# A layer with a matrix scan on one core: the block solver's loads, places and priority, and products between merge pieces

## The chip, the cores and the metric

The kernel runs on one core of a Trainium2 chip. The core has TensorE (PE, with its weight loads as PEld), VectorE (DVE), ScalarE (ACT), GpSimd (POOL) and SyncE (SP), which here only issues transfers; 16 DMA engines move the data. The metric is the device time of one execution in microseconds.

## The reference

One layer over 1024 latent tokens and 256 context tokens of width 1024, all in 32-bit floats:

```
h  = modulate(rms_norm(x, norm1_g), sh1, sc1)          # also for the context
u  = h @ w_in                                           # 512 Fourier columns, 1920 RWKV columns
r, k, v = conv1d_centred(u[rkv]); decay, a = low-rank maps; kk = normalised k
for each time step, direction and head (2 x 8, state 64 x 64):
    sa = s @ kk_t
    s  = s * w_t - sa kk_t a_t + v_t k_t
    y  = s @ r_t                                        # context tokens first, no readout there
rw  = (group_norm(y) + bonus) * gate
out = concat(fourier_mix(u[:512]), rw) @ w_out;  x = x + g1 * out
h2  = modulate(rms_norm(x, norm2_g), sh2, sc2)
x   = x + g2 * (silu(gate) * val) @ w_down              # gate, val = 3x3 grid convolution of h2 @ w_up
return rms_norm(x, final_g)
```

The scan over time is a chain: a state depends on the one before.

## The kernel before, in words

**Scan in chunks.** The 1280 time steps are cut into 20 chunks of 64 (the first four are the context), worked as `step(s)` for s = 0 to 19, each over 16 pairs of direction and head. Inside a chunk the recurrence is a triangular system. Its inverse `z` (64 x 64 a chunk and pair) is found outside the chain, for a *block* of four chunks at a time: `solve(b)` inverts the 32 x 32 diagonal parts on VectorE, with 128 of them side by side, one in each partition, by 30 rounds of two instructions (L853, L854); `merge(b)` puts the two 32 x 32 halves together on PE in four pieces (two at L874, two at L883), each read out by ScalarE (L877, L886). Blocks 0 to 4 serve steps 0-3, 4-7 and so on. `prep(s)` (L939) applies `z` to the inputs of step s. A step is: `pw` (L957), its copy (L959), `py` (L964), `pS` (L973), the state update on VectorE (add L975, multiply L977), the second part of `py` (L982). Between them stand the two halves of `prep(s+1)`.

**The solver's data.** The preparation writes the scores to DRAM (`xad`), rows first. `solve(b)` loads them into `n` with the row in the partition, by four transfers (L843, L844: rows of 64 or 32 floats); VectorE turns them (L848) into `arr`, where a partition holds one matrix; after the rounds it turns the inverse back twice (L858, L859). `n` alternates between two pools (`wks[b % 2]`); `arr` has one place, in `wks[0]`. `merge` needs `n` and `arr`.

**Preparation.** The input projection runs in products of 128 columns (`product`, L197, into `plat`, two places of two PSUM banks). After each, generators in `self.sides` hand out small pieces in turn, two a product part (`tick`): the norm of `k` (`norms`), the transposes of `v` (`turns`), and the pair work that makes the scan's inputs (`pair`, `scores`). Each yields a PE instruction; PE's order is the order of tracing here. The preparation has two PSUM pools one after the other (`s1a`, `s1b`), and `plat` is in both. The first solve is interleaved with the last pair by hand.

**What sets the order.** A planner orders each engine's instructions when the program is built: it runs a picture of time with its own costs and takes, among what is ready, what has the best priority; priority goes by the order of tracing unless `prio` shifts it. `behind(i)` and `paced` tie an instruction to stand behind another one on its own engine. In `weave` the scan's chain and a *fill* (the remaining Fourier products, then the Fourier transform and its output projection) are traced with a far better priority (`-AHEAD`), and PE's instructions of both are tied into one fixed order (`self.link`): the plan's numbers say how many fill pieces follow each step. In `chain` the next block's solver is traced a few rounds at a time behind the step's parts, with the same priority; in steps 2, 6, 10 (and 14) its rest is finished, and the merge pieces stand between the step's parts, with no fill between them.

**After the scan.** `heads_out` and `out_pieces` (with `second_norm`, which writes `h2` through `v2`, a small buffer of four places) run in steps 14 to 19; then come the feed-forward products (`ffn_up`, `down_round`).

Of the kernel before, what the change touches and what calls it, by code (L numbers as in the profile page):

```python
# [10 lines left out]
F32 = mybir.dt.float32  # L11
F32R = mybir.dt.float32r
AF = mybir.ActivationFunctionType
OP = mybir.AluOpType
# [149 lines left out]
class B:  # L164
# [63 lines left out]
    def weave(self, a, b, fill=(), plan=()):  # L228
# [5 lines left out]
        while True:  # L234
# [76 lines left out]
    def stage0(self, wk, hT, first, rest):  # L311
# [64 lines left out]
        us = [(pp.tile([128, T], F32, name="plat", bufs=2), pp.tile([128, TC], F32, name="pctx", bufs=2)) for m in first]  # L376
# [77 lines left out]
    def post_k(self, us, m):  # L454
# [7 lines left out]
        def norms():  # L462
            nc.scalar.activation(kk, k, AF.Square, scale=self.kk_[:, p:p + 1])
            for b, n in BLOCKS:
# [12 lines left out]
    def post_v(self, us, m):  # L477
        nc, wk = self.nc, self.wk
# [6 lines left out]

        def turns():
            for d in range(2):
                for b0 in (0, 4, 8):
                    nb = min(4, 10 - b0)
                    x = v[:, b0 * 128:(b0 + nb) * 128]  # L490
                    if d:
                        vr = wk.tile([128, 512], F32, name="vrev", tag="vt", bufs=2)
                        nc.vector.tensor_copy(vr[:, :nb * 128], rev(v[:, TT - (b0 + nb) * 128:TT - b0 * 128]))
                        x = vr
                    vt = wk.tile([128, 4, 128], F32, name="vt", bufs=2)
                    aux = self.pp.tile([128, 512], F32, name="aux")
                    for b in range(nb):
                        i = nc.tensor.transpose(aux[:, b * 128:(b + 1) * 128], x[:, b * 128:(b + 1) * 128], self.ident)
                    nc.scalar.activation(vt[:, :nb], aux[:, :nb * 128].rearrange("p (b c) -> p b c", c=128), AF.Copy)
                    t0 = b0 if d else (b0 + 2) % 10  # L500
                    for h in range(2):
                        nc.sync.dma_start(rows[d, h, :, t0:t0 + nb], vt[:, :nb, 64 * h:64 * h + 64])
                    yield i
# [191 lines left out]
    def fourier_first(self, hT):  # L695
# [5 lines left out]
        for j in range(2):  # L701
# [3 lines left out]
            us.append(self.pp.tile([128, T], F32, name="plat", bufs=2))  # L705
# [3 lines left out]
    def fourier_rest(self, hT, wk, us):  # L709
# [10 lines left out]
        for j in range(2, 4):  # L720
# [4 lines left out]
            ps = self.pp.tile([128, T], F32, name="plat", bufs=2)  # L725
# [99 lines left out]
    def gate_rows(self, pool):  # L825
# [5 lines left out]
        nc.gpsimd.tensor_add(gb, gb, t)  # L831
        return gb


    def solve(self, b):


# [665 lines left out]
```

## Time and profile before

| | |
|---|---|
| time, median of 3 runs | 1714.73 us (1708.97 to 1720.9) |
| profiled execution | 1714.45 us |
| its span, first to last instruction | 1712.7 us |
| instructions | 29106 |
| PE, PEld busy | 89%, 72% |
| VectorE, ScalarE, GpSimd busy | 66%, 41%, 30% |
| mean granted PE clock | 0.931 |
| DMA traffic | 246.29 MB in 208919 packets |

A busy share is that of the whole span. "L957" is line 957 of the kernel. A row such as "PE pw L957 <- DVE SV L977" says that PE sat idle ahead of line 957 until VectorE's line 977 released it. The granted clock is the share of full speed at which PE was let run. In a group, the columns after the bar are the busy time, the mean of one in ns, and the idle time just before.

### The profile page before, as it was taken

To read this page: it belongs to the slowest core of one execution; us is meant where nothing else is said; L and a number is where in the kernel's file an instruction comes from. 1 tells how busy PE (TensorE), PEld (TensorE's weight loads), DVE (VectorE), ACT (ScalarE), POOL (GpSimd) and SP (SyncE) were. 2 spreads that over 40 slices of the span, in tenths; PEclk is the share of its full clock that TensorE was granted. 3 is DMA by queue.
4 is the path that set the end of the run, shared out by engine and by line. 5 is a ranking of instruction groups with operands and counts; after the bars stand their busy time and mean duration, and the time that the engine had idled before them with its cause. 6 is when DMAs were issued, how large, how long until landed. Compare 5 with 4: busy or idle time off the path is not lost. (4 is left out here: it accounts for less than half of the span.)

```text
span 1712.7 us, 29106 instructions
## 1 busy us (share of the span) xinstructions
PE 1520.9 (89%) x11642; PEld 1229.8 (72%) x11642; DVE 1129.6 (66%) x1604; ACT 702.2 (41%) x1193; POOL 507.4 (30%) x443
## 2 busy tenths in 40 slices
PE   4998898888977768899897999999999998999996
PEld 3786676665656566778676888888888886787785
DVE  3614745665596685866557599999999999515613
ACT  3433545556443334423666422222222223435533
POOL 0013523443332134301215122222222223354454
PEclk7999998999988777789999999999999999999998
DMA  8577757767778667564620311111111115434532
GB/s 313 201 287 214 227 165 215 230 184 231 177 215 178 160 164 173 179 174 140 191 95 16 116 39 48 50 50 49 50 50 50 49 50 185 158 124 138 195 124 98
DMA packets 208919, 246.29 MB, mean 144 GB/s; under 512 B 53238, under 2 KB 162944, under 8 KB 208784
## 3 DMA queue, kind: packets, MB, share of 16 engines
q1 hardware_dynamic: 202608, 233.92, 45.1%
q0 software_dynamic: 6176, 10.51, 2.2%
q8 instruction: 92, 1.51, 0.4%
q14 instruction: 43, 0.35, 0.1%
HBM read 177.99 MB, written 66.33 MB: 143 GB/s over the span
## 5 line engine op out<-in xcount | busy, mean ns | idle before, releaser
L189 POOL TENSOR_TENSOR wlo<-wraw,whi 128x1024 fp32r<-128x1024 f32 x105 | 253.0, 2411 | 656.9 <-ACT whi L188 656.9
L1223 DVE SCALAR_TENSOR_TENSOR conv<-u,c_fcw,conv 128x945 f32<-128x945 f32 (+2 forms) x344 | 411.5, 1219 | 36.2 <-ACT conv L1216 28.1
L188 ACT ACTIVATE whi<-wraw 128x1024 fp32r<-128x1024 f32 x123 | 129.4, 1052 | 301.5 <-issue 165.8
L197 PE MATMUL u<-h2h,wlo 128*128 128x512 f32 x672 | 206.9, 389 | 0.0
L197 PE MATMUL u<-h2h,whi 128*128 128x512 f32 x672 | 206.9, 389 | 0.0
L197 PE MATMUL u<-h2l,whi 128*128 128x512 f32 x672 | 206.8, 389 | 0.0
L189 DVE TENSOR_TENSOR al<-act,ah 128x256 fp32r<-128x256 f32 (+1 forms) x88 | 62.7, 716 | 137.8 <-ACT ah L188 137.5
L197 PEld LDWEIGHTS u<-h2h,wlo 128*128 128x128 f32 x672 | 126.1, 188 | 26.2
L197 PEld LDWEIGHTS u<-h2l,whi 128*128 128x128 f32 x672 | 126.1, 188 | 26.1
L197 PEld LDWEIGHTS u<-h2h,whi 128*128 128x128 f32 x672 | 126.1, 188 | 26.2
L1280 PE MATMUL e<-wlo,ah 128*128 128x512 f32 x264 | 103.0, 390 | 2.8 <-POOL wlo L189 2.8
L197 PE MATMUL plat<-hTh,whi 128*128 128x512 f32 x272 | 99.6, 447 | 4.5 <-DVE v L451 4.5
L188 ACT ACTIVATE ah<-act 128x256 fp32r<-128x256 f32 (+1 forms) x88 | 45.9, 523 | 139.6 <-PE e L1280 99.3
L1280 PE MATMUL e<-whi,al 128*128 128x512 f32 x264 | 103.0, 390 | 0.0
L197 PE MATMUL plat<-hTl,whi 128*128 128x512 f32 x272 | 90.8, 415 | 0.0
L197 PE MATMUL plat<-hTh,wlo 128*128 128x512 f32 x272 | 90.0, 412 | 0.5 <-DVE wlo L668 0.5
L916 POOL COPY WV<-SV 64x512 f32<-64x512 f32 x40 | 26.6, 666 | 146.4 <-ACT xs L941 45.6
L1280 PE MATMUL e<-whi,ah 128*128 128x512 f32 x264 | 67.0, 389 | 0.0
L559 DVE TENSOR_TENSOR_SCAN cs<-c_rst,sg 128x256 f32<-128x256 f32 x40 | 31.0, 776 | 50.1 <-ACT sg L543 45.8
L197 PEld LDWEIGHTS plat<-hTh,wlo 128*128 128x128 f32 x272 | 53.6, 198 | 13.6 <-DVE wlo L668 0.9
L634 PEld LDWEIGHTS aux<-x,bk 64*128 64x128 f32 x640 | 46.1, 207 | 24.0 <-issue 12.5
L197 PEld LDWEIGHTS plat<-hTh,whi 128*128 128x128 f32 x272 | 47.1, 195 | 22.2 <-issue 14.1
(292 smaller groups left out, 3134.1 us busy)
## 6 DMA issues: line engine op xcount, KB each, us to landing
wraw<-wd SPq DMA_DIRECT2D x66, 512.0 KB
ad<-ada SPq DMA_DIRECT2D x12, 2048.0 KB
wraw<-wu SPq DMA_DIRECT2D x42, 512.0 KB
xrd<-x SPq DMA_DIRECT2D x32, 640.0 KB
xs<-xrd SPq DMA_DIRECT2D x16, 1280.0 KB
xad<-x SPq DMA_DIRECT2D x80, 192.0 KB
xs<-xad SPq DMA_DIRECT2D x18, 512.0 KB
kvb<-kvd SPq DMA_DIRECT2D x16, 512.0 KB
```

The lines of the kernel that those rows point to most:

```text
L188: self.nc.scalar.activation(hi, x, AF.Copy)
L189: (lo_eng or self.nc.gpsimd).tensor_sub(lo, x, hi.bitcast(F32))
L197: mm = self.nc.tensor.matmul(ps[:, b:b + n], wt[:, k, :], xt[:, k, b:b + n], start=k == 0 and i == 0, stop=k == 7 and i == 2)
L559: nc.vector.tensor_tensor_scan(cs, self.rst, o(sg), 0.0, op0=OP.mult, op1=OP.add)
L634: i = nc.tensor.matmul(ps[h][:, c, :64 * w], bk(c, h), x[R[h], c, 1:6 * w - 4:6], start=True, stop=True)
L916: nc.gpsimd.tensor_copy(wv[r, h], sv[r, h])
L1223: nc.vector.scalar_tensor_tensor(og[:, R, Cc], ug[:, Ri, Ci], self.fcw[:, m, w:w + 1], og[:, R, Cc], op0=OP.mult, op1=OP.add)
L1280: nc.tensor.matmul(t, x[:, 128 * (i - i0):128 * (i - i0) + 128], w[:, j, 512 * (b - b0):512 * (b - b0) + 512], start=k == 0 and m == 0, st ...
```

## The change

**Preparation.** `plat` moves to a PSUM pool of its own (`s1p`) that lives through both halves. `norms` hands over its turn once between the square and the first product. `turns` makes the reversed copy of the next piece before it works on the present one, and its buffers (`vt` and `vrev` together) have four places instead of two.

**Solver.** `arr` is loaded directly, one matrix in a partition, by four transfers with rows of 32 floats, and lies in `wks[b % 2]`, like `n`. The opening transpose is gone. After the rounds, `solved(b)` loads the part of `n` that `merge` still needs (two transfers) and does the two closing transposes. The loads of blocks 1 and 2 are traced between the input loads of steps 0, 1 and 2, those of block 3 at the end of step 2, and of block 4 at the end of step 6. `solving(b, i)` traces all rounds at once with a worse priority than all else (`+AHEAD // 2`), behind the update of step 0, 3 or 7 (block 1: at the chain's start).

**Merge steps.** After each merge piece of steps 2, 6 and 10 the chain says "mid", and `weave` puts the plan's next number of fill pieces there; the plan's sums are as before (19 and 52 pieces).

**Room.** `tab` has four places instead of six; the raw output weights are taken from the Fourier transform's pool; `v2` takes `arr`'s place in `wks[1]`, as one tile of four pieces.

```diff
-            if i == "end":
+            if i in ("mid", "end"):
                 self.burst(fill, next(plan, 0))
...
-        ul = self.pp.tile([128, T], F32, name="plat", bufs=2)
+        ul = self.pl.tile([128, T], F32, name="plat", bufs=2)
...
             nc.scalar.activation(kk, k, AF.Square, scale=self.kk_[:, p:p + 1])
+            yield self.pace[-1]
...
+        def turned(b0, nb):
+            vr = self.wv.tile([128, 512], F32, name="vrev", tag="vt", bufs=4)
+            nc.vector.tensor_copy(vr[:, :nb * 128], rev(v[:, TT - (b0 + nb) * 128:TT - b0 * 128]))
+            return vr
+
         def turns():
...
+            for j, (d, b0, nb) in enumerate(pieces):
+                x = vr if d else v[:, b0 * 128:(b0 + nb) * 128]
+                if j + 1 < len(pieces) and pieces[j + 1][0]:
+                    vr = turned(*pieces[j + 1][1:])
+                vt = self.wv.tile([128, 4, 128], F32, name="vt", bufs=4)
...
-                    tab = wk.tile([128, 2, 258], F32R, name="tab", bufs=6)
+                    tab = wk.tile([128, 2, 258], F32R, name="tab", bufs=4)
...
+    def solve_load(self, b):
+        src = self.xad[b].rearrange("p i q f -> (i q) p f")
+        arr = self.arrs[b] = self.wks[b % 2].tile([128, 32, 32], F32, name="arr")
+        for h in range(2):
+            for g in range(2):
+                r = slice(64 * h + 32 * g, 64 * h + 32 * g + 32)
+                self.nc.sync.dma_start(arr[r], src[:, r, 192 * h + 32 * g:192 * h + 32 * g + 32])
+
     def solve(self, b):
-        n = self.wks[b % 2].tile([128, 32, 64], F32, name="n")
...
-        diag = n[:, :, 0:32]
-        arr = self.wks[0].tile([128, 32, 32], F32, name="arr")
-        nc.vector.transpose(arr.rearrange("p a b -> p b a"), diag.rearrange("p m c -> p c m"))
+        nc, arr = self.nc, self.arrs[b]
         for j in range(1, 31):
...
+    def solved(self, b):
+        nc, arr = self.nc, self.arrs[b]
+        n = self.wks[b % 2].tile([128, 32, 64], F32, name="n")
+        src = self.xad[b].rearrange("p i q f -> p (i q) f")
+        for h in range(2):
+            nc.sync.dma_start(n[64 * h:64 * h + 32, :, 32:64], src[64 * h:64 * h + 32, :, 192 * h + 32:192 * h + 64])
+        diag = n[:, :, 0:32]
         nc.vector.transpose(diag.rearrange("p m c -> p c m"), arr)
         nc.vector.transpose(arr, diag)
...
+    def solving(self, b, i):
+        with self.prio(by=AHEAD // 2), self.behind(i):
+            for _ in self.solve(b):
+                pass
...
             yield from self.merge(0)
-            self.ahead = self.solve(1)
         for s in range(4) if not a else (4,) if a == 4 else ():
             self.load_x(s)
+            if s < 2:
+                self.solve_load(s + 1)
         if a in (0, 4):
             yield from self.prep(a)
+        if not a:
+            self.solving(1, None)
...
                 elif s % 4 == 2:
                     if not n:
-                        for _ in self.more:
-                            pass
+                        self.solved(g)
                         self.more = self.merge(g)
                     else:
-                        yield from islice(self.more, 1)
-                elif n >= late and left:
-                    left -= 1
-                    next(self.more, None)
-            for _ in range(left):
-                next(self.more, None)
+                        for i in islice(self.more, 1):
+                            yield i
+                            yield "mid"
             if s % 4 == 2 and s < 14:
-                yield from self.more
-                self.ahead = self.solve(g + 1)
-                next(self.ahead)
+                for i in self.more:
+                    yield i
+                    yield "mid"
+                if g < 3:
+                    self.solve_load(g + 2)
+            if s in (0, 3, 7):
+                self.solving(g + 1, self.updated)
             yield "end"
...
-            v = wk.tile([128, 2, 128], F32, name="v2", bufs=4)
+            if o % 4 == 0:
+                vs = self.wks[1].tile([128, 4, 2, 128], F32, name="v2", tag="arr")
+            v = vs[:, o % 4]
...
-                b.weave(0, 4, fill, (7, 6, 6))
+                b.weave(0, 4, fill, (7, 4, 4, 1, 1, 1, 1))
...
-            b.weave(4, 14, fill, (0, 0, 4, 5, 4, 5, 1, 8, 8, 9, 8))
+            b.weave(4, 14, fill, (0, 2, 3, 1, 1, 1, 1, 1, 4, 4, 1, 2, 2, 2, 2, 0, 8, 9, 8))
```

More of the change, by code (lines that the diff above doesn't have):

```diff
@@ L375, in stage0 @@
             modulation(q, ads[q])
-        us = [(pp.tile([128, T], F32, name="plat", bufs=2), pp.tile([128, TC], F32, name="pctx", bufs=2)) for m in first]
+        us = [(self.pl.tile([128, T], F32, name="plat", bufs=2), pp.tile([128, TC], F32, name="pctx", bufs=2)) for m in first]
         for n, (b, w) in enumerate(BLOCKS):
@@ L724, in fourier_rest @@
                 side.append(more)
-            ps = self.pp.tile([128, T], F32, name="plat", bufs=2)
+            ps = self.pl.tile([128, T], F32, name="plat", bufs=2)
             for k in range(8):
@@ L863, in solve, with first_solve @@
         self.zs[b] = n, arr
+    def first_solve(self):
+        self.solve_load(0)
+        yield
+        yield from self.solve(0)
+        self.solved(0)
     def merge(self, b):
@@ L999, in chain @@
             yield from self.merge(0)
-            self.ahead = self.solve(1)
         for s in range(4) if not a else (4,) if a == 4 else ():
             self.load_x(s)
+            if s < 2:
+                self.solve_load(s + 1)
         if a in (0, 4):
             yield from self.prep(a)
+        if not a:
+            self.solving(1, None)
         for s in range(a, b):
             g = (s + 1) // 4 + 1
-            if s in (0, 3, 7, 11):
-                self.more, self.share = self.ahead, 9 if not s else 6
-            late, left = 3 if s >= 4 else 2, self.share if s % 4 != 2 and s < 14 else 0
             if s > 14 and s % 2 == 0:
@@ L1062, in loads @@
                     yield
-        return w, loads()
+        return w, loads
     def out_pieces(self, w, hs, x, n):
@@ L1330, in build @@
             b.wp = pool("w", st)
+            b.pl = pool("s1p", st, space=PSUM)
             s1, s1k = ExitStack(), ExitStack()
@@ L1359, in build @@
                 b.bank = b.pp, "aux"
-                b.first = b.solve(0)
+                b.first = b.first_solve()
                 pairs = b.pairs()
@@ L1399, in fill @@
                 with ExitStack() as st:
-                    for n, i in enumerate(b.fourier_out(pool("fo", st, side="right"))):
+                    fo = pool("fo", st, side="right")
+                    parts = loads(fo)
+                    for n, i in enumerate(b.fourier_out(fo)):
                         yield i
                         if n % 2:
-                            next(loads, None)
-                b.out_all(loads)
+                            next(parts, None)
+                    b.out_all(parts)
                 x1 = b.x1 = pool("x1", tail, side="right").tile([128, 8, T], F32, name="x1")
```

60 lines of the change are left out of this document (22 added, 38 removed).

## The prediction

> **What bounds the kernel now.** The page comes first, for the span and the engines' shares.
>
> ```profile
> span 1712.7 us, 29106 instructions
> PE 1520.9 (89%) x11642; PEld 1229.8 (72%) x11642; DVE 1129.6 (66%) x1604; ACT 702.2 (41%) x1193; POOL 507.4 (30%) x443
> ```
>
> TensorE (PE) is busy for 89% of the span, so about 192 us of it are idle, and what a change can win is PE's idle time and its time at a lower clock. To find both I cut the span into stretches at the points where the kernel's work changes: preparation to 470, its end with the first solve, the scan from 529 (its merge steps in windows of their own), then the heads, then the feed-forward part. The columns are: length, busy time of PE, PEld, VectorE (DVE), ScalarE (ACT) and GpSimd (POOL) with instruction counts, granted clock, DMA share, GB/s.
>
> ```profile
> 90.00:470.00 380.00, 334.01 (x2366) 249.59 (x2365) 200.15 (x302) 195.13 (x396) 134.59 (x159) 0.93 0.72 216
> 470.00:529.00 59.00, 44.45 (x298) 34.07 (x296) 55.29 (x117) 22.71 (x61) 21.66 (x29) 0.80 0.77 214
> 529.00:575.00 46.00, 33.38 (x559) 27.78 (x560) 32.00 (x77) 13.84 (x32) 5.88 (x11) 0.85 0.51 102
> 575.00:603.00 28.00, 19.09 (x460) 16.51 (x460) 9.18 (x13) 12.13 (x26) 6.99 (x11) 0.70 1.02 254
> 603.00:636.00 33.00, 21.11 (x359) 18.85 (x355) 29.67 (x68) 11.39 (x21) 12.23 (x16) 0.79 0.52 140
> 636.00:662.00 26.00, 24.09 (x444) 22.13 (x444) 8.39 (x12) 13.07 (x26) 16.25 (x22) 0.54 0.97 215
> 662.00:710.00 48.00, 38.67 (x571) 30.44 (x569) 42.86 (x98) 19.81 (x41) 9.51 (x12) 0.92 0.56 161
> 710.00:743.00 33.00, 31.09 (x468) 27.25 (x470) 11.97 (x21) 11.32 (x20) 9.05 (x14) 0.65 0.85 224
> 743.00:830.00 87.00, 78.35 (x1172) 63.47 (x1170) 58.89 (x118) 35.05 (x58) 15.66 (x18) 0.94 0.54 163
> 830.00:980.00 150.00, 130.99 (x1331) 115.43 (x1328) 85.59 (x161) 88.28 (x141) 36.12 (x42) 0.97 0.26 82
> 980.00:1713.00 733.00, 704.47 (x3070) 575.24 (x3069) 549.31 (x527) 240.58 (x309) 232.46 (x106) 0.99 0.27 89
> ```
>
> The last 733 us have PE busy at clock 0.99, and the change touches nothing there. Three things stand out before. From 90 to 470 PE loses 46 us while no other engine is near full. From 470 to 529 VectorE is busy 55.29 of 59 us: there it is the bound. In the scan PE idles with VectorE high (603 to 636: 21.11 against 29.67 us of 33), and in the two merge stretches (636 to 662, 710 to 743) it is the reverse: PE busy nearly all the time at clock 0.54 and 0.65, so those stretches are long because the clock is low. The next view is what PE waits for, in the preparation (first five rows) and in the scan from 529 to 830: total, times, longest.
>
> ```profile
> PE aux L498 <- DVE vrev L493: 13.6, 4, 5.6
> PE aux L466 <- ACT kk L463: 5.9, 3, 2.1
> PE aux L634 <- DVE x L636: 4.7, 2, 2.9
> PE aux L644 <- DVE x L636: 4.5, 3, 2.4
> PE plat L197 <- DVE v L451: 4.5, 1, 4.5
> ...
> PE pw L957 <- DVE SV L977: 13.5, 7, 7.6
> PE aux L681 <- DVE fu L678: 7.6, 1, 7.6
> PE po L781 <- ACT sqf L780: 5.8, 2, 5.5
> PE po L1075 <- DVE x L1080: 3.8, 1, 3.8
> PE z L883 <- ACT n L877: 3.4, 3, 1.9
> PE z L874 <- ACT n L877: 1.9, 1, 1.9
> PE pz L939 <- DVE SV L975: 1.7, 1, 1.7
> ```
>
> In the scan the waits end at VectorE. What VectorE does meanwhile is the solver: one solve (529 to 575) by its groups, with the idle time ahead of each.
>
> ```profile
> L853 DVE TENSOR_TENSOR arrt<-arr 128x30 f32<-128x30 f32 (+14 forms) x30 | 11.1, 369 | 1.0
> L854 DVE TENSOR_TENSOR arr<-arr,arrt 128x30 f32<-128x30 f32 (+14 forms) x30 | 9.9, 331 | 0.9
> ...
> L848 DVE STREAM_TRANSPOSE arr<-n 128x1024 f32<-128x1024 f32 x1 | 2.2, 2161 | 11.5 <-PE pz L939 11.5
> L858 DVE STREAM_TRANSPOSE n<-arr 128x1024 f32<-128x1024 f32 x1 | 2.0, 2021 | 0.0
> L859 DVE STREAM_TRANSPOSE arr<-n 128x1024 f32<-128x1024 f32 x1 | 1.2, 1246 | 0.0
> ```
>
> That is 11.1 + 9.9 + 2.2 + 2.0 + 1.2 = 26.4 us of VectorE per solve, at the same priority as the scan's own updates (L975, L977), which stand behind up to a whole run of it in the queue.
>
> **The change part by part.** The profiled execution took 1714.45 us (span 1712.7 and 1.75 around it), 0.3 us from the median 1714.73; the sum is made against it.
>
> *A. Preparation to 470.* The reversed copy of `v` is made one piece ahead with four places for it instead of two: it aims at the 13.6 us. One more turn between the squares and the product that reads them aims at the 5.9 us. `plat` in a pool of its own, which lives through both halves of the preparation, lets the product after the pool change start in the other place: 4.5 us. Together 24.0 us at most. The extra turn costs nothing by itself, since the pair that follows is held by `v`, not by the norms. But PE's order is fixed, and the pair chain behind these stalls (the waits on L636: 4.7 + 4.5 us) has used them to catch up; what is late next is that chain. Bounds 0 and 24; I take a little over half: −13.
>
> *B. 470 to 529.* VectorE is the bound, and the first solve loses its opening transpose (L848, 2.2 us). The pair work stays. −2, bounds 0 and −4.
>
> *C. 529 to 575.* Before, the second solve's transpose sat idle for 11.5 us, as its array shared one place with the first. With two places it can begin when its rows have landed, and it loses the 2.2 us. The gain is up to 13.7 us; but the merge in step 2 still needs the whole solve, VectorE has 32.0 us of work in this stretch, and the loads come no earlier. The 7.6 us wait on `fu` lies in here and is not counted again. −5, bounds 0 and −13.7.
>
> *D. 603 to 830.* With the solver at low priority the planner puts its instructions only where nothing else of VectorE is ready. The waits that stood behind it: 13.5 + 5.8 + 3.8 + 1.7 = 24.8 us. One solver instruction (0.33 to 0.37 us) can still be ahead of an update each time; eleven waits by 0.35 us make 3.9, which leaves 21. −20, bounds −8 (where the planner's picture of free time is off) and −25. The third, fourth and fifth solve have four to seven steps each, so I cost their delay at nothing; the cover is VectorE's free time (the windows from 529 to 830 add up to 193 of 301 us busy); if it is gone, the merge waits, which is the last rival.
>
> *E. Products between merge pieces.* The waits between pieces, 3.4 + 1.9 = 5.3 us, now hold a product each. The number of products is the same; they only move from the step's end into it. −4, bounds 0 and −5.3.
>
> *F. The clock.* The same 32 matmuls of L973 took, in a merge step and outside one:
>
> ```profile
> 709.04 0.47 PE L957 MATMUL pw<-SV,xs 128*64 128x64 f32 x2 [2.27 <-DVE SV L977]
> ...
> 719.45 1.97 PE L973 MATMUL pS<-WV,xs 128*64 128x64 f32 x32
> ...
> 745.83 1.15 PE L973 MATMUL pS<-WV,xs 128*64 128x64 f32 x32
> ...
> 715.00:720.00 5.00, 5.00 (x120) 4.54 (x116) 1.91 (x5) 2.81 (x5) 1.03 (x2) 0.50 0.11 24
> ```
>
> At clock 0.50 they take 1.97 instead of 1.15 us: 42% of such time is lost. The gap of 2.27 us stands at the entry of the slow stretch, and then five full microseconds of small matmuls do not bring the clock back. Taking the clock as 1.0 or 0.5, the two merge stretches hold 2 × 0.46 × 26 + 2 × 0.35 × 33 = 47 us at half rate, PE busy 55.18 of 59, so 47 × 0.94 × 0.42 = 18 us are lost. D removes the gap at the entry, and the products moved in are large matmuls. But one product a piece may not keep the clock up. I take half, with a little for the merge before 603: −10. Bounds 0, and 29 if all the half-rate time of 575 to 743 goes (2 × (0.30 × 28 + 0.21 × 33 + 0.46 × 26 + 0.08 × 48 + 0.35 × 33) = 85 us, PE busy 134.05 of 168, so 85 × 0.80 × 0.42 = 29).
>
> *G. Heads, 830 to 980.* `v2` now takes one place of four pieces instead of four places, so the second four wait until the first four are read.
>
> ```profile
> L1194 DVE SCALAR_TENSOR_TENSOR v<-x,G,rs x16: 476/480/487, 938.9 to 966.8; 128x256 f32<-128x256 f32 x16
> ```
>
> Three such changes lie on the path (the last two tile pairs); each can drain at most about two instructions of 0.48 us: 0 to +3, I take +1, because three other pieces cover the first one's way through ScalarE. Fewer places for `tab` (four for six) and the raw weights in another pool I cost at nothing, as no wait of PE on these loads is among the scan's waits; in a gap they would cost what a wait of the list costs, 1 to 2 us.
>
> *H. The loads.* Every block came in four DMAs:
>
> ```profile
> n<-xad SPq DMA_DIRECT2D x10, 256.0 KB
> n<-xad SPq DMA_DIRECT2D x10, 128.0 KB
> ...
> q1 hardware_dynamic: 202608, 233.92, 45.1%
> ```
>
> By the code these are 1024 rows of 256 B or 128 B each, 4096 rows a block. Now four DMAs of 1024 rows of 128 B fill `arr` and two more the rest of `n`: 6144 rows, the same bytes. The queue's mean is 0.451 × 16 × 1712.7 / 202608 = 61 ns of one DMA engine per packet, so 2048 more rows cost 7.8 us of all sixteen. At the scan's start it is more: the third block's 4096 rows now come there too, on SP's queue between the scan inputs of steps 0 to 3 and the `v` rows, which queue behind them. 6144 × 61 / 16 = 23 us if all of it is exposed, 0 if hidden. DMA share from 529 to 575 is 0.51, so I take +3. The Trainium skill speaks against such rows: "DMA: Bandwidth & Descriptors", section "Why small descriptors are slow (HBM only)", gives a fixed overhead of about 3 cycles a packet beside one for every 32 bytes. An estimate from that page: 2048 × 11 + 2048 × 7 cycles a block before, 6144 × 7 now, 17% more where I count half more rows as half more time; by it H would be about +1. No row here separates the two sizes.
>
> Sum: −13 − 2 − 5 − 20 − 4 − 10 + 1 + 3 = −50, so 1664.5 us.
>
> **The rivals.** *The clock holds through the whole scan.* Once no gap of several microseconds is left, the rate never falls: F is −29 in place of −10, and the preparation (clock 0.93, so 2 × 0.07 × 380 = 53 us at half rate, of which 53 × 0.88 × 0.42 = 20 us are lost) gives some 8 more. −77: 1637. Against it, the row at 709.04: a gap of 2.27 us came at the edge of a slow stretch, and gaps of 2 us will remain; and 715 to 720. The Trainium skill, "TensorE: Matmul & The Clock Gate", section "Part 1: The HAM clock gate (the "warmup" mystery)", has the rate fall after an idle window of about 3.4 us and return after about 3.4 us of sustained work, which would bear this case out; the trace disagrees on the return, with PE busy 5.00 of 5 us at 0.50.
>
> *The stalls go, the clock stays, the start hangs on the loads.* F 0 and H +23: −50 + 10 + 20 = −20, 1694. For it: DMA share 1.02 from 575 to 603 and the rows above. Against it: 0.51 before that.
>
> *The planner leaves the solver where it was.* Low priority orders only what is ready together; if VectorE is free in the planner's picture at the same moments, nothing moves in the scan. Then only A and B stay, less half of H: 1702. Against it: the second place alone changes when the solve is ready.
>
> *Slower: the solver comes late.* PE meets the merge in a fixed order. A solver that yields to everything may end after its merge's place, and PE then stands empty for the rest of it, up to 11.1 + 9.9 + 2.0 + 1.2 = 24.2 us at each of the steps 2, 6, 10 and 14. Two full waits eat the −50; from the third on the kernel is slower: 1664 + 73 = 1737. For it: step 2 has only two steps of time, and VectorE is the bound up to 529. Against it: the other three have twice that and more.
>
> **How the numbers follow.** Chances: the forecast (1644 to 1681 by the milder and harsher halves of A, C, D and F) 0.52; clock holds 0.12; stalls go but the start hangs 0.18; solver stays 0.10; late solver 0.08. A difference of about 1% (17 us) is what a measurement of this kernel can tell from no change. Faster than that, below 1697.6: the forecast, the clock case and two thirds of the third case, 0.76; within 1%: the rest of that and the fourth, 0.16; slower 0.08. The range for 8 in 10 leaves out the late solver, half of the fourth case and the far end of the clock case: 1630 to 1702. Likeliest 1664.
>
> **What would show it.** A: the waits L498, L466 and `plat` on L451 gone, the scan's first merge near 514 in place of 529. C: the second solve's first product ahead of 540. D: no wait of PE over 1 us on SV, `fu` or `x` L1080. E, F: clock above 0.8 in the merge stretches, large products between the small pieces. H: DMA share above 1 at the scan's start and PE waiting for `xs` would show the third case. The prediction is wrong if merge pieces wait for VectorE's transposes (late solver), or if the scan from first merge to last is not at least 25 us shorter.

## The result, and the profile after

The changed kernel took 1667.87 us (median of 4 executions, 1663.5 to 1671.63), the kernel before, run beside it, 1711.85 us (1708.53 to 1720.9). The ratio is 0.973, 95% interval 0.969 to 0.978. The forecast was 1664 us, in a range of 1630 to 1702. The total came out as forecast, but not by the sum's terms: the preparation gave about twice what was written down for it, the scan little more than half, and the mechanism of the largest term (low priority) turned out to gain no time that could be measured.

The profiled execution took 1667.14 us. From its page, the span, the engines' shares and SyncE's hardware queue:

```profile
span 1665.4 us, 29094 instructions
...
PE 1490.0 (89%) x11642; PEld 1204.9 (72%) x11642; DVE 1123.4 (67%) x1599; ACT 703.0 (42%) x1193; POOL 511.1 (31%) x443
...
q1 hardware_dynamic: 213008, 233.92, 45.6%
```

TensorE has the same 11642 matmuls, and its busy time fell by 1520.9 − 1490.0 = 30.9 us: that much of the 47.3 us of span is a higher clock and shorter matmuls, the other 16.4 us are idle time. The stretches below are cut at the same points of the work as those of before (the preparation, its end, then at the scan's steps 2, 4, 6, 7, 10 and 11, the rest of the scan, the heads, the feed-forward part); the columns are those of the prediction.

```profile
90.00:443.00 353.00, 326.07 (x2422) 246.50 (x2420) 202.86 (x301) 195.78 (x399) 137.84 (x159) 0.97 0.77 232
443.00:502.00 59.00, 43.56 (x306) 33.51 (x306) 51.82 (x117) 24.08 (x64) 21.06 (x29) 0.83 0.83 225
502.00:541.00 39.00, 29.82 (x534) 24.85 (x534) 29.15 (x74) 13.33 (x29) 7.72 (x12) 0.82 0.63 130
541.00:576.00 35.00, 22.26 (x478) 18.13 (x479) 32.01 (x80) 12.76 (x28) 4.63 (x9) 0.80 0.65 166
576.00:618.00 42.00, 24.86 (x372) 21.90 (x372) 32.83 (x70) 14.85 (x29) 21.74 (x28) 0.72 0.65 184
618.00:639.00 21.00, 18.11 (x454) 14.96 (x454) 8.39 (x12) 13.82 (x25) 9.53 (x13) 1.00 0.86 204
639.00:671.00 32.00, 30.61 (x546) 25.75 (x547) 30.31 (x72) 14.89 (x31) 6.13 (x8) 1.00 0.78 223
671.00:702.00 31.00, 24.81 (x458) 19.92 (x458) 21.68 (x45) 11.74 (x21) 11.14 (x16) 0.89 0.72 225
702.00:783.00 81.00, 76.63 (x1191) 63.20 (x1188) 34.16 (x53) 36.48 (x61) 15.99 (x19) 0.96 0.57 178
783.00:932.00 149.00, 130.52 (x1327) 114.19 (x1326) 85.04 (x161) 87.15 (x139) 38.95 (x42) 0.97 0.27 86
932.00:1665.00 733.00, 704.73 (x3072) 575.62 (x3070) 548.80 (x526) 241.01 (x309) 231.16 (x105) 0.99 0.27 89
```

| stretch | before, us | after, us | difference |
|---|---|---|---|
| 90 to the end of the preparation's main part | 380 | 353 | −27 |
| its end with the first solve | 59 | 59 | 0 |
| scan, first merge to step 4 | 74 | 74 | 0 |
| scan, steps 4 to 10 | 140 | 126 | −14 |
| then to the heads | 87 | 81 | −6 |
| heads, feed-forward part | 883 | 882 | −1 |

In the preparation PE's idle time fell from 46 us to 353.00 − 326.07 = 27 us, and its busy time by 8 us at a clock of 0.97 for 0.93. In the scan the two merge steps that stood at clock 0.54 and 0.65 are at 1.00 (618 to 639) and 0.89 (671 to 702). And there is a loss: from 541 to 618 VectorE is busy 64.8 of 77 us and PE only 47.1. What PE waits for, in the preparation (90 to 470, the largest row) and then in the scan (502 to 783); total, times, longest:

```profile
PE aux L542 <- DVE x L640: 5.5, 5, 1.8
```

```profile
PE po L765 <- DMA tab<-dft: 12.7, 1, 12.7
PE pz L958 <- DVE arr L857: 8.3, 1, 8.3
PE pS L992 <- ACT WV L978: 6.2, 6, 4.1
PE po L1099 <- ACT cH L188: 5.9, 1, 5.9
PE pz L958 <- DMA xs<-xrd: 3.5, 1, 3.5
...
PE pw L976 <- DVE SV L996: 1.2, 3, 0.6
```

Most of the old stalls are gone (on `vrev` 13.6, on `plat` 4.5, on `kk` 5.9, of which rows at other products still show 3.1; in the scan 13.5 on the update of `SV`, now 1.2). Three new ones stand in the scan's steps 3 to 5, 12.7 + 8.3 + 3.5 = 24.5 us.

### The profile page after: what moved, and what is told of

Same layout as the page of the kernel before. It is cut to its first block, busy times and chain, and to the rows that moved or that the text cites. A ratio compares the mean times of both kernels' runs of the same rounds, so it can differ in the third digit from the quotient of the medians.

```text
span 1665.4 us, 29094 instructions
## 1 busy us (share of the span) xinstructions
PE 1490.0 (89%) x11642; PEld 1204.9 (72%) x11642; DVE 1123.4 (67%) x1599; ACT 703.0 (42%) x1193; POOL 511.1 (31%) x443
## 3 DMA queue, kind: packets, MB, share of 16 engines
q1 hardware_dynamic: 213008, 233.92, 45.6%
## 5 line engine op out<-in xcount | busy, mean ns | idle before, releaser
L189 POOL TENSOR_TENSOR wlo<-wraw,whi 128x1024 fp32r<-128x1024 f32 x105 | 254.6, 2426 | 667.6 <-ACT whi L188 630.2
L935 POOL COPY WV<-SV 64x512 f32<-64x512 f32 x40 | 27.9, 698 | 122.7 <-ACT xs L960 41.1
L856 DVE TENSOR_TENSOR arrt<-arr 128x30 f32<-128x30 f32 (+9 forms) x150 | 52.8, 352 | 14.7 <-DMA arr<-xad 10.6
L197 PEld LDWEIGHTS plat<-hTl,whi 128*128 128x128 f32 x272 | 52.1, 194 | 14.1 <-issue 2.4
L958 PE MATMUL pz<-xs,n 64*64 64x128 f32 (+1 forms) x576 | 43.1, 294 | 21.0 <-DVE arr L857 8.3
```

The lines of the kernel that those rows point to most:

```text
L189: (lo_eng or self.nc.gpsimd).tensor_sub(lo, x, hi.bitcast(F32))
L197: mm = self.nc.tensor.matmul(ps[:, b:b + n], wt[:, k, :], xt[:, k, b:b + n], start=k == 0 and i == 0, stop=k == 7 and i == 2)
L856: nc.vector.tensor_tensor(tv, arr[:, 0:j, j:j + 1].to_broadcast(sh), arr[:, j:j + 1, j + 1:].to_broadcast(sh), op=OP.mult)
L935: nc.gpsimd.tensor_copy(wv[r, h], sv[r, h])
L958: mm = nc.tensor.matmul(ps[r, i, :w], z[r, q + i, :], src[h][:, i], start=True, stop=True)
```

## The experiments

The lines below give the median, the range of the executions of each (4; for `plat` alone 10, for the turns alone 9), and the ratio to the kernel before, run beside it, with its 95% interval. Where a kernel's own profile is used, two marks cut it: the start of the first merge, and the first product of 512 columns of the feed-forward part (before: 529.0 and 979.4, so the scan with the heads is 450.4; after: 501.9 and 931.8, so 429.9).

**The three preparation edits alone.** The kernel before with `plat` in a pool of its own, the extra turn in `norms`, and `turns` one piece ahead with four places.

> The kernel before with the three edits of the preparation alone. Theory 1 (the trace after, where the scan's first merge stands at 501.9 in place of 529.0): the preparation gives 27 us, the scan the remaining 20; this kernel takes about 1685 us and its first merge stands at 502 to 504. Rival (the prediction's terms): the preparation gives 13 to 15 us, about 1698 us, and the rest of the shift comes from the solver's missing transpose and load.

Measured: 1686.44 us (1683.26 to 1687.83), ratio 0.983 (0.980 to 0.985). These edits are worth some 29 us (1.7% of 1714). The first merge starts at 508.4, and the scan with the heads takes 445.8 us: in its profile 20.6 us are won ahead of the first merge, 4.6 us in the scan. The time is that of the first theory, though the merge starts later than the 502 to 504 it named. The prediction had 13 for these edits.

**Each of the three alone.**

```diff
-        ul = self.pp.tile([128, T], F32, name="plat", bufs=2)
+        ul = self.pl.tile([128, T], F32, name="plat", bufs=2)
```

> The kernel before with the PSUM pool of plat alone. The three edits of the preparation together gave 28 us. Theory: each gives its own wait and the clock that falls behind it; this one 4.5 us of wait, so 4 to 8 us shorter than before. Rival: the edits only pay together, since the next wait takes the place; within 3 us of before.

```diff
             nc.scalar.activation(kk, k, AF.Square, scale=self.kk_[:, p:p + 1])
+            yield self.pace[-1]
```

> The kernel before with the extra turn in the norms alone. Theory: its own waits of 5.9 us and the clock, 4 to 9 us shorter than before. Rival: within 3 us of before.

```diff
-                        vr = wk.tile([128, 512], F32, name="vrev", tag="vt", bufs=2)
...
+                if j + 1 < len(pieces) and pieces[j + 1][0]:
+                    vr = turned(*pieces[j + 1][1:])
+                vt = self.wv.tile([128, 4, 128], F32, name="vt", bufs=4)
```

> The kernel before with the transposes of v alone (reversed copy one piece ahead, four places). Theory: its own waits of 13.6 us and the clock behind them, 12 to 20 us shorter than before. Rival: about half of the wait, 5 to 8 us, since the pair chain uses the same stalls.

Measured against the waits that they aim at:

| edit | wait of before | PE idle, 90 to 440 | clock there | median | ratio (95%) |
|---|---|---|---|---|---|
| none | – | 42.2 | 0.93 | – | 1 |
| `plat` | 4.5 | 38.3 | 0.94 | 1709.58 | 0.996 (0.994 to 0.997) |
| turns | 13.6 | 36.4 | 0.94 | 1709.51 | 0.995 (0.993 to 0.997) |
| extra turn | 5.9 | 33.6 | 0.95 | 1697.75 | 0.989 (0.986 to 0.993) |
| all three | 24.0 | 25.0 | 0.97 | 1686.44 | 0.983 (0.980 to 0.985) |

The idle time is 350 us less PE's busy time in the window. Its rows for the kernel before, the one with the extra turn alone and the one with all three:

```profile
90.00:440.00 350.00, 307.76 (x2192) 229.75 (x2191) 185.95 (x277) 180.40 (x362) 125.17 (x145) 0.93 0.71 219
```

```profile
90.00:440.00 350.00, 316.38 (x2327) 241.14 (x2326) 187.89 (x279) 190.31 (x380) 128.61 (x147) 0.95 0.74 223
```

```profile
90.00:440.00 350.00, 324.99 (x2415) 246.82 (x2417) 198.36 (x296) 194.67 (x389) 135.81 (x154) 0.97 0.76 230
```

In the same 350 us PE gets 2192, 2327 and 2415 matmuls done. The list of waits is a poor price list: the largest wait (13.6) bought 5.8 us of idle time, the 5.9 us one 8.6 us. Where the rest of the 13.6 us went isn't shown by one row: PE's waits on `x`, the pair chain to which the prediction feared they would be handed on, sum to 20.7 us in the kernel before and 21.1 us with the turns edit (90 to 520). A shorter idle time goes with a higher clock: the means of the `plat` matmuls of 512 columns fell from 451, 419 and 415 ns to 436, 409 and 401 ns (all three edits), about 3%. The turns edit came nearer to its rival, and the extra turn gave more than twice what was expected of it. Why that one is worth some 19 us of time when it frees 8.6 us of PE in this window isn't settled: in its profile 6.2 us are won ahead of the first merge and 7.7 us in the scan, which it doesn't touch.

**The priority.** The changed kernel with the solver at the scan's own priority.

```diff
-        with self.prio(by=AHEAD // 2), self.behind(i):
+        with self.behind(i):
```

> The kernel after with the solver's rounds at the scan's own priority, still traced in one run behind the updates of steps 0, 3 and 7. Theory (D): the whole run of about 21 us stands ahead of the next update, three times in the scan; 25 to 60 us longer than after, about 1695 to 1728 us. Rival: the planner finds the same places whatever the priority; within 5 us of after.

Measured: 1668.23 us (1667.11 to 1673.11), ratio 0.972 (0.970 to 0.975): the same as the changed kernel. Its waits in the scan are the same ones, and none on `SV` is among the first:

```profile
PE po L765 <- DMA tab<-dft: 13.4, 1, 13.4
PE pS L992 <- ACT WV L978: 7.0, 9, 3.4
PE pz L958 <- DVE arrt L856: 6.8, 1, 6.8
```

So the time doesn't hang on the low priority. (By the code, `prio` sets the count back after each traced piece, so rounds traced in one run of some 60 instructions may still rank behind an update; the edit takes away `AHEAD // 2`, and not every difference in rank.)

**The new places, without priority and without products between merge pieces.** The preparation edits, the direct loads into two places and the room that they need, on the kernel before: the solver's rounds dealt out by hand at the scan's priority, and the old fill plan.

```diff
+        yield from self.solve(b)
+        self.solved(b)
...
+            if s < 2:
+                self.solve_load(s + 1)
...
-                self.ahead = self.solve(g + 1)
-                next(self.ahead)
+                if g < 3:
+                    self.solve_load(g + 2)
+                self.ahead = self.whole(g + 1)
```

> The preparation's edits, and of the solver's only the direct loads into two places (at the points where after has them) with the same room; the solver interleaved by hand at the scan's priority and the fill plan as before, no products between merge pieces. Theory: VectorE's waits in the scan came from the solver's opening instruction standing at the head of its queue for rows that land later than planned (21.2 us in 3 waits before); with rows that land early no wait of PE on SV over 2 us is left, and the scan from the first merge to the first full feed-forward product is 428 to 436 us (before 450, with the preparation's edits alone 446): about 1670 to 1677 us. Rival: the interleaving itself holds the updates up, waits on SV stay near 13 us in sum, 442 to 448 us of scan, 1682 to 1690 us.

Measured: 1669.19 us (1659.86 to 1671.85), ratio 0.971 (0.968 to 0.975): all of the changed kernel's gain, and apart from the preparation edits' own 0.980 to 0.985. Its scan with the heads takes 425.8 us, the one of the preparation edits alone 445.8 (the profile here is of the fastest of the four executions, so the medians' difference of 17 us is the better figure). The time is a little better than the theory's, but the theory's own sign failed: it wanted no wait of PE on `SV` over 2 us, and there are 9.2 us of them with one of 7.0, nearer to the 13 of the rival, in which the interleaving itself holds the updates up.

```profile
PE pw L981 <- DVE SV L1001: 9.2, 4, 7.0
```

What the places did change are VectorE's waits for rows. First in the preparation edits alone: VectorE's waits in the scan, the last use of block 0's `n` by the inputs of a step, and the loads of blocks 2 and 4 on SyncE's queue.

```profile
DVE arr L852 <- DMA n<-xad: 27.4, 4, 11.6
```

```profile
L943 PE MATMUL pz<-y,n x64: 218/218/366, 542.3 to 560.9; 64*64 64x64 f32 x64
```

```profile
570.23 0.58 SPq L847 DMA_DIRECT2D n<-xad  x1
...
702.98 0.60 SPq L847 DMA_DIRECT2D n<-xad  x1
```

And the same two views with the loads into places of their own (loads of blocks 2 and 4):

```profile
DVE arrt L856 <- DMA arr<-xad: 11.0, 2, 6.3
```

```profile
515.56 3.96 SPq L847 DMA_DIRECT2D arr<-xad  x4
...
624.98 3.56 SPq L847 DMA_DIRECT2D arr<-xad  x4
```

With the old layout the rows land in `n`, the very tile from which the steps read the finished inverse; so block 2's rows can come only when block 0's last step has used it (560.9), 570.2 − 508.4 = 62 us after the first merge. The opening transpose then stands at the head of VectorE's queue and waits, 27.4 us in four blocks, with all updates behind it. With the rows in `arr`, which is free as soon as the merge two blocks back has read it, block 2's load is issued 515.6 − 499.8 = 16 us after the first merge, block 4's 125 us after it instead of 195, and the waits are 11.0.

That this is where the 17 us come from is not shown. The starts of the steps, in us after the first merge, put the gain elsewhere:

| | step 3 | step 5 | step 10 | step 11 | feed-forward |
|---|---|---|---|---|---|
| before | 61.2 | 89.5 | 180.0 | 213.8 | 450.4 |
| preparation edits alone | 59.1 | 88.9 | 172.8 | 211.0 | 445.8 |
| with the new places | 59.0 | 86.9 | 170.6 | 198.5 | 425.8 |
| changed kernel | 53.5 | 98.4 | 169.1 | 200.4 | 429.9 |

Up to step 10, with three of the four waits for rows behind it, the kernel with the new places is 2.2 us ahead of the preparation edits alone. Step 10 gives another 10 us (38.3 to 27.9). With the preparation edits alone PE stands there 9.33 us for ScalarE's copy of a merge piece, which waits behind a copy of `cH` for a transfer of the Fourier result (692.74).

```profile
695.37 1.92 PE L878 MATMUL z<-n 32*32 32x32 f32 x64 [9.33 <-ACT n L881]
```

Step 11, behind the fourth wait for rows, gives 3.5 us. How the new places shorten step 10 stays open.

**The same, with the loads issued in the program where the kernel before issues them.** This was meant to tell the early issue from the layout.

```diff
+        self.solve_load(b)
+        yield
         yield from self.solve(b)
...
-            if s < 2:
-                self.solve_load(s + 1)
...
-                if g < 3:
-                    self.solve_load(g + 2)
                 self.ahead = self.whole(g + 1)
+                next(self.ahead)
```

> The kernel before with the three preparation edits and the solver's blocks loaded in its own layout into two places, as in the run that measured 1669.2, but each block's load issued where the kernel before issues its load (at the first round of solving in step 0, and at the ends of steps 2, 6 and 10) instead of a block ahead. Theory (what the scan gains comes from the rows being in place when the solver's first instruction reaches the head of VectorE's queue): the waits of VectorE's first rounds on the rows are back, 15 to 30 us in all over four blocks, and the median is 1680 to 1690, near the 1686.4 of the preparation edits alone. Rival (the gain comes from the layout: no opening transpose, half the bytes to wait for): 1666 to 1674, with waits on the rows under 8 us in all.

Measured: 1676.96 us (1672.62 to 1678.65), ratio 0.976 (0.973 to 0.979): between the two expectations, and its interval overlaps that of the run before it. The edit did not do what it says. The planner moved the loads forward by itself: those of blocks 2, 3 and 4 are issued 16, 72 and 129 us after the first merge, against 16, 68 and 125 with the loads traced early and 62, 123 and 195 with the old layout. Only block 1 comes later (first round 9.4 us after the first merge, not 5.0; then 10.0 us of PE's waiting on `fu`, not 6.6). So where a load stands in the program matters little here; when its place comes free decides. The two possible causes (early rows, no opening transpose) were not taken apart by this run.

**The old layout in the changed kernel.** Rows first into `n`, opening transpose, loads one block ahead, solving behind steps 3, 7 and 11, at low priority.

```diff
-        arr = self.arrs[b] = self.wks[b % 2].tile([128, 32, 32], F32, name="arr")
+        n = self.ns[b] = self.wks[b % 2].tile([128, 32, 64], F32, name="n")
...
+        nc.vector.transpose(arr.rearrange("p a b -> p b a"), self.ns[b][:, :, 0:32].rearrange("p m c -> p c m"))
...
-            if s in (0, 3, 7):
-                self.solving(g + 1, self.updated)
+            if s in (3, 7, 11):
+                self.solving(g, self.updated)
```

> The kernel after with the solver's old loads: rows first into n, opening transpose on VectorE, one block ahead only (block 2 from step 2, 3 from 6, 4 from 10); low priority, two places for arr and the products between merge pieces stay. Theory: priority and products make the scan's gain and the direct load nothing; SP's queue is free ahead of step 4, where after has a wait of 8.35 us; 0 to 10 us shorter than after, 1658 to 1668 us. Rival (C): the direct load and the earlier start are needed, merges wait for late solves; 8 to 25 us longer, 1676 to 1693 us.

Measured: 1677.28 us (1675.05 to 1685.54), ratio 0.979 (0.975 to 0.982), 9 us more than the changed kernel, as its rival said, though the intervals overlap (0.969 to 0.978); it is just apart from the run with the scan's priority (0.970 to 0.975). PE's longest wait is at the first merge piece of step 10 (it starts at 695.2, right behind the closing transpose of 693.2): this is the late solver of the prediction's last rival, once instead of at every merge.

```profile
PE z L893 <- DVE n L870: 16.1, 1, 16.1
```

**No products between the merge pieces.** The changed kernel with all pieces behind the steps: the plan's numbers of a merge step are added up.

```diff
-            if i in ("mid", "end"):
+            if i == "mid":
+                continue
+            if i == "end":
                 self.burst(fill, next(plan, 0))
```

> The kernel after with no products between merge pieces: the same number of them stands at the step's end. Theory (E and F of the prediction): merge steps 6 and 10 fall to half clock again, 8 to 15 us longer than after, about 1678 us. Rival: the solver's low priority alone removes the gaps at which the clock falls; within 4 us of after.

Measured: 1673.59 us (1672.14 to 1681.17), ratio 0.977 (0.973 to 0.980): 5.7 us more than the changed kernel, with overlapping intervals, and the merge steps don't fall to half clock as the theory said. In the step with the second merge the clock is 0.63 with the preparation edits alone, 0.51 with the new places alone, 0.80 without products between the pieces, and 1.00 in the changed kernel (618 to 639, above):

```profile
615.00:642.00 27.00, 23.59 (x450) 21.31 (x452) 9.27 (x10) 13.20 (x25) 18.22 (x24) 0.63 0.95 229
```

```profile
605.50:633.00 27.50, 23.14 (x411) 21.32 (x412) 12.43 (x24) 12.82 (x25) 15.59 (x24) 0.51 0.81 207
```

```profile
624.00:649.00 25.00, 21.00 (x453) 18.40 (x452) 8.30 (x12) 13.93 (x25) 10.41 (x15) 0.80 0.78 204
681.00:708.00 27.00, 23.55 (x478) 19.80 (x478) 21.80 (x46) 12.45 (x23) 12.41 (x18) 1.00 0.78 247
```

In the step with the third merge it is the other way round (1.00 in 27 us here, 0.89 in 31 us in the changed kernel). So the products between pieces go with a higher clock at one merge and not at each, and their sum, 5.7 us by the medians, isn't clear of noise.

**Where steps 3 to 5 lose the gain.** Through step 2 the changed kernel is ahead by 8 us, at step 4 by nothing (74 us from the first merge in both), and at step 5 it is 9 us behind. Its GpSimd and SyncE queues there, and VectorE's groups from 541 to 618:

```profile
575.19 1.28 POOL L935 COPY WV<-SV 64x512 f32<-64x512 f32 x2 [24.34 <-DMA SV<-vd]
...
590.18 2.87 POOL L761 DMA_DIRECT2D tab<-dft  x4
```

```profile
554.39 1.01 SPq L922 DMA_DIRECT2D xs<-xad  x2
555.53 7.36 SPq L847 DMA_DIRECT2D arr<-xad  x4
562.93 1.38 SPq L923 DMA_DIRECT2D xs<-xrd  x2
```

```profile
L857 DVE TENSOR_TENSOR arr<-arr,arrt 128x58 f32<-128x58 f32 (+14 forms) x59 | 22.6, 382 | 1.9
L856 DVE TENSOR_TENSOR arrt<-arr 128x84 f32<-128x84 f32 (+14 forms) x58 | 22.2, 383 | 1.7
```

Step 4's second input rows stand behind block 3's loads on SyncE's queue, and the table `tab` behind GpSimd's copies of `SV`, which wait for their rows (24.34). The row "PE pz L958 <- DVE arr L857: 8.3" names VectorE, but that product doesn't read `arr`; it reads `xs`, whose last rows are issued at 562.93, so it is more likely a wait for them. Meanwhile VectorE works off two solves back to back, 59 rounds. Three kernels move these things: the fill's pieces behind steps 4 and 5, block 3's loads and solving to step 4's end, and both.

```diff
-            b.weave(4, 14, fill, (0, 2, 3, 1, 1, 1, 1, 1, 4, 4, 1, 2, 2, 2, 2, 0, 8, 9, 8))
+            b.weave(4, 14, fill, (0, 0, 5, 1, 1, 1, 1, 1, 4, 4, 1, 2, 2, 2, 2, 0, 8, 9, 8))
```

> The changed kernel with one thing moved: of the feed of products, the pieces behind steps 4 and 5 are dealt out as 0 and 5 instead of 2 and 3, so that the first use of the table tab comes one step later. In the changed kernel's trace TensorE waits 12.7 us once for that table (issued on GpSimd's queue at 590.2, wanted near 584). Theory (the wait is on the path and is what the scan's steps 3 to 5 lose of the gain of steps 0 to 2): the row of that wait is gone or under 3 us, and the median is 6 to 12 us below the changed kernel's 1667.9, 1656 to 1662. Rival (VectorE, busy 28.2 of the 30 us around it with the third block's solving, sets the pace there, and TensorE's wait costs nothing): the wait is gone, another one stands on VectorE's tiles in steps 4 to 7, and the median is within 4 us of 1668.

Measured: 1669.94 us (1668.03 to 1674.14), ratio 0.973 (0.969 to 0.976), the same as the changed kernel. Both expectations took it for granted that the wait on `tab` would go, and it did not: it moved behind the pieces. And 6.7 us on `SV` are back (longest 5.2), which in the changed kernel fell into the wait for the table.

```profile
PE po L765 <- DMA tab<-dft: 12.0, 1, 12.0
```

```diff
-                if g < 3:
-                    self.solve_load(g + 2)
-            if s in (0, 3, 7):
-                self.solving(g + 1, self.updated)
+            if s in (4, 7):
+                self.solve_load((s + 1) // 4 + 2)
+            if s in (0, 4, 7):
+                self.solving(3 if s == 4 else g + 1, self.updated)
```

> The changed kernel with the third block's loads and its solving moved from the ends of steps 2 and 3 to the end of step 4, behind step 4's own input rows, and the last block's loads to the end of step 7. In the changed kernel's trace the product of step 4 waits 8.3 us, and its rows xs stand on SyncE's queue behind four loads of the solver's rows that are 7.4 us in being issued (555.5 to 562.9). Theory (those loads delay step 4): the wait of 8.3 us is gone, and the median is 4 to 8 us below 1667.9, 1660 to 1664. Rival (the third solve now comes late, since it has to be done before step 7's first product): a wait of over 5 us on the solver's tiles in front of the merge behind step 6, and the median 1668 to 1676.

Measured: 1665.86 us (1663.47 to 1668.13), ratio 0.970 (0.967 to 0.973). The wait of 8.3 us is gone and 4.4 us on `pl` have come; no wait on the third solve appears. The scan with the heads is 422.3 us, 7.6 less than in the changed kernel's profile, but the median is only 2 us lower and the intervals overlap.

Both edits together:

> Both moves of the two kernels before it. If both waits (12.7 us for the table, 8.3 us for step 4's rows) are on the path and apart from each other, their costs add: 1648 to 1656. If VectorE's solving sets the pace of steps 4 to 6 either way, 1664 to 1672. If the late third solve decides, 1668 to 1678.

Measured: 1663.52 us (1660.23 to 1669.08), ratio 0.968 (0.965 to 0.972). Its waits in the scan:

```profile
PE pz L958 <- ACT xs L960: 9.7, 7, 7.3
PE po L765 <- DMA tab<-dft: 7.8, 1, 7.8
PE po L1099 <- ACT cH L188: 5.9, 1, 5.9
PE pz L958 <- DVE pl L189: 4.4, 1, 4.4
```

Its scan with the heads takes 420.8 us, 9.1 less than after, and it has the lowest median of all; against the changed kernel's 0.969 to 0.978 that is no more than likely. The two costs did not add up: the waits of 21 us became others of 22, among them 7.3 us on a copy of ScalarE. This fits the case in which VectorE sets the pace there (from 545 to 622, the same part of the scan, its busy time is 63.80 of 77 us, in the changed kernel 32.01 + 32.83 = 64.84 of 77), but no run lightened VectorE itself, so it isn't shown.

```profile
545.00:622.00 77.00, 52.53 (x1060) 45.36 (x1060) 63.80 (x148) 32.08 (x63) 30.34 (x42) 0.78 0.80 210
```

## Why the prediction was right, and where it was not

**A, preparation: undersized by half (−13 forecast; −29 by the three edits alone, −27 in the stretch to 470).** The step that failed is "I take a little over half" of the listed waits, with no term for the clock. Idle time fell by 19 us, within the bounds 0 to 24, and 8 us came from the clock (0.93 to 0.97). Those 8 us did stand in the prediction, as part of the rival in which the clock holds; they belonged into A, which with them went beyond its bound of −24. The condition named (first merge near 514) was passed: 501.9.

**B (−2): 0.** VectorE's busy time in that stretch fell from 55.3 to 51.8 us, more than the transpose's 2.2, and the stretch still takes 59 us.

**C (−5): 0 as seen at step 4.** The second solve's rounds do start earlier (509.7, where the kernel before began its opening transpose at 540.6; counted from the first merge 7.8 us for 11.6), short of the 11.5 us that the wait promised: it now waits 7.7 us for its rows. Steps 0 to 2 win 8 us in the changed kernel, and steps 3 to 5 give them back; the new places alone win nothing there (step 3 at 59.0 for 59.1 us).

**D (−20): the waits went from the list, but the mechanism was wrong.** The waits on `SV`, `fu` and `x` did go (13.5 to 1.2 on `SV`). But the step "with the solver at low priority the planner puts its instructions only where nothing else of VectorE is ready" fell. At the scan's own priority the time is the same, and at low priority the solver's rounds still stand in front of the update. The next rows run from the end of step 4's `pS` to the start of its update, in the kernel before, with the new places alone, and in the changed kernel; in all three VectorE (third busy time) works on nothing but the solver there:

```profile
608.57:616.07 7.50, 2.17 (x48) 1.86 (x48) 6.85 (x20) 1.32 (x3) 0.00 (x0) 0.82 0.28 72
```

```profile
577.36:584.28 6.92, 2.17 (x48) 1.86 (x48) 6.28 (x19) 1.32 (x3) 0.00 (x0) 0.85 0.30 78
```

```profile
581.42:586.33 4.91, 2.22 (x50) 1.86 (x48) 4.57 (x12) 1.39 (x3) 1.44 (x2) 0.98 0.26 74
```

In the first two PE waits 7.6 and 7.0 us for that update. In the changed kernel the update is late too, but PE stands at the table `tab` meanwhile (12.7 us), so the wait isn't listed; with the table's pieces moved, 5.2 us of it appear. The second thing that D had wrong is the price: the kernel with the new places keeps 9.2 us on `SV` and 6.6 on `fu` and is as fast as the changed one, which has 1.2 and 0.9 and pays 24.5 us of new waits in steps 3 to 5.

Waits for rows were in it as well, one instruction at the head of VectorE's queue with all else behind it. The kernel before shows it in one row, from 530 to 540, where VectorE does nothing at all:

```profile
530.00:540.00 10.00, 5.54 (x236) 5.03 (x230) 0.00 (x0) 5.00 (x9) 3.10 (x6) 0.74 1.24 216
```

C had read this very wait as one for the place of `arr` only. Its rows can't have been in place either, since the last of their loads is issued at 533.54; with the preparation edits alone the same wait (11.57 us) is put down to the rows. Ahead of the 7.6 us on `SV` the same instruction had waited 4.40 us for rows, so an estimate of what the rounds alone made of it is 3.2 us; but with the new places nothing waits for rows there, and 7.0 us remain. The condition set in the prediction, a scan at least 25 us shorter from the first merge to the last, was missed: it is 19.9 us shorter (274.5 to 254.6), 20.5 with the heads. By its own sign the prediction was wrong there.

**E and F (−4 and −10): together −10 in the profile's merge steps, −5.7 by the experiment, not clear of noise.** By the starts of their first products, step 2 went from 15.5 to 14.1 us, step 6 from 27.2 to 21.1 and step 10 from 33.8 to 31.3. The clock is above 0.8 in the merge steps, as E and F demanded. But the products are not the whole reason (0.80 and 1.00 without them), and neither are the new places (0.51 and 0.88 with them alone). The experiment bears out at most half of the 14 us of E and F, and what else raised the clock stays open.

**G (+1): 0.** The heads take 149 us for 150.

**H (+3): another place, another size.** No stretch shown of the scan's start has a DMA share above 1, so the rival in which the start hangs on the loads did not happen in full; but its mechanism did, in step 4, through the order on SyncE's queue (7.36 us of issuing in front of `xs`). The price per row was wrong: q1 has 213008 − 202608 = 10400 packets more for the same 233.92 MB, and its packets' time went from 0.451 × 16 × 1712.7 = 12359 us to 0.456 × 16 × 1665.4 = 12151 us. At 61 ns each it should have risen by 634 us. The Trainium skill, "DMA: Bandwidth & Descriptors", section "Why small descriptors are slow (HBM only)", from which the prediction had estimated +1, is nearer to this; the trace shows no rise at all.

**The rivals.** The clock held in the merge steps but not through the scan (0.72 from 576 to 618), so 1637 was too far. "The planner leaves the solver where it was" was right that priority gains nothing, and wrong about the time; its own last sentence, that the second place changes when the solve is ready, names what the runs bear out. The late solver was real, and came once when the loads were put back into `n`.

In sum the preparation (A and B, −15 forecast, −27 in the profile) was 12 us better than its terms and the scan with the heads (C to H, −35 forecast, −20.5 in the profile) some 15 us worse. The point is right because these cancel, which is luck: A lay beyond its own bound. The split itself is good to some us only, since the first merge of kernels with the same preparation starts anywhere from 499.8 to 508.8 us, and the profile used here (501.9) is an early one.

## What to carry to other kernels

Ask of a load when its destination's place comes free: with a place of its own, and not in the tile from which the last result is still read, the rows here were issued 46 to 70 us earlier, and the kernel was 17 us faster. Then ask where those 17 us stand: the theory that led to the edit named a wait of which two thirds stayed (13.7 to 9.2 us on `SV`), and most of the gain was in another step. A list of waits tells where an engine stood, not what removing a wait gains: a late result can hide behind another wait, and what is really gone can come back with interest through the clock. When a total comes out as forecast, test the terms alone; here the mechanism of the largest one was worth nothing.

## What was not expected of the hardware

Small matmuls can run at the full rate. In the changed kernel's second merge step, 21 us at clock 1.00, the 64 small matmuls of a merge piece take 1.20 us, with six of 258 columns behind each of the first two pieces:

```profile
620.04 1.20 PE L893 MATMUL z<-n 32*32 32x32 f32 x64
```

Without products between the pieces the third merge step reached 1.00 as well, so large matmuls are not the condition. Gaps of 1.07 and 1.09 us inside this step did not lower it. What brings the rate down, and when it comes back, stays open: in the kernel before it was at 0.50 through 5 us of unbroken work.

The first merge starts anywhere from 499.8 to 508.8 us in the profiles of the eight kernels whose preparation and first solve are those of the changed kernel. What moves it isn't known, and it is as much as any of the last experiments wanted to tell apart.
